# A hybrid attention and FFN block: MLA slots taken in pairs, with the heads' transposes two heads ahead

## The chip, the cores and the metric

The kernel runs on one core of a Trainium2 chip. The metric is the device time of one execution in microseconds (us), the median over several runs. A profile of one execution comes beside it. The engines are TensorE (PE: products and transposes, with its weight loads as PEld), VectorE (DVE), ScalarE (ACT), GpSimd (POOL) and SyncE (SP, which issues most loads). L158 is line 158 of the kernel.

## The reference

One layer on 512 tokens of width 1024, in float32. A normalised x is multiplied by W_in, whose columns feed two groups of attention heads: eight MLA heads, whose queries and keys come out of small latent vectors, and four differential heads. Both attend under a mask by chunks of 64 tokens. A gated FFN with a short convolution and a gated embedding follow. What concerns the change is the MLA group:

```python
    q = rms_norm(q, q_g)
    k = rms_norm(k, k_g)
...
        logits = jnp.einsum('bhqd,bhkd->bhqk', qb, k_t).astype(jnp.float32) * scale
        logits = jnp.where(allowed[None, None], logits, NEG_INF)
        probs = jax.nn.softmax(logits, axis=-1).astype(v_t.dtype)
        return jnp.einsum('bhqk,bhkd->bhqd', probs, v_t)
```

Eight heads (queries and keys of 96 columns, values of 64), and for each the queries in four blocks of 128 tokens. The mask lets block t see the keys of blocks 0 to t only.

## The kernel before, in words

**Number format.** Wide products are made of three: each operand is split into a rounded high part and a low remainder, and `mm3` (L154 to L159) adds high x high, high x low and low x high. A split costs an ACT cast (high) and a DVE subtraction (low): `split` at L182, `lo` at L304, `load_w` at L145.

**MLA slots.** A slot is a head and a query block, (h, t), 32 in all, in the order of `slots` (L727). A slot has these steps:

- `mla_logits` (L564): three products into a `lg` bank, n = 128 (t + 1) columns wide; a DVE maximum over the row and a product with the query's norm; an ACT exponential into a `pm` tile, with the row sum.
- `probs_T` (L535): t + 1 transposes of `pm` into a `tp` bank, then a copy of the bank into a `pt` tile, by DVE for even t and by ACT for odd t.
- `mla_pv` (L578): one product per key block (two records each in the trace) with V, into the bank `mo` of the head pair. After the last slot of a head pair DVE divides by the row sums into `ym`.

Queries and keys of a head are transposed by `mla_q` and `mla_k` (L548, L555) into a `tp` bank and split from there into `QT[h % 2]`: two sets for eight heads.

**Buffers.** PSUM (L112) has banks `acc` 2, `lg` 3, `tp` 2 and `ob` 1. In SBUF there are four `pm` tiles (PM = 4, L50), two `pt` tiles (L124) and five of each weight half (NW = 5). A tile or bank of a tag can be written again once the last reader of the one that held it is done.

**Filling.** `zd_units` (L405) is a generator with 48 units of six products each, the differential group's part of x W_in. `pump(n)` issues the next n. Its first 16 units use the `acc` and `lg` banks ahead of the slots, the others two `acc` banks in turn; after each full sum ACT copies the bank out (L392) and, for queries and keys, squares the tile (L396), and DVE sums the squares (L397). The weights of the second group are loaded by `z1_hi` (L469), the last of them inside the slot loop.

**Order of the work.** PE's instructions run in the order in which the program writes them, throughout (L98). DVE, ACT and POOL do so only inside `region` (L217), which ends in the slot loop at i = 4 (L740); after that a planner orders them by priority and by when their inputs come free. `tc.issue_after(x)` puts what is written inside it behind instruction x on that engine. The loop before takes one slot at a time (L734 to L772): logits of the next slot, in two of four slots the transposes of the next head's queries or keys, one filling unit, the transposes of this slot, the V product of the last one.

**After the slots.** In head 7 the filling changes to the first w_out products (`wo_units`, L642), and `last_mla` (L721) brings the differential group's first transposes (`diff_T`), the transposes of the MLA output (`y_split`) and the loads of x into the last four slots. The differential slots follow (L779).

Of the kernel before, what the change touches and what calls it, by code (L numbers as in the profile page):

```python
# [12 lines left out]
F32R = mybir.dt.float32r  # L13
I32 = mybir.dt.int32
AF = mybir.ActivationFunctionType
ALU = mybir.AluOpType
# [4 lines left out]
P = 128  # L21
T = 512
NT = 4
# [4 lines left out]
H = 8  # L28
# [26 lines left out]
NW = 5  # L55
# [3 lines left out]
FILL_KV = (0, 1, 1, 1)  # L59
FILL_UQ = (1, 1, 1, 1)  # L60
FILL_QK = 5
FILL_MLA = (1, 1, 1, 1)
FILL_DIFF = ((2, 1, 1, 1), (1, 1, 2, 1), (1, 2, 2, 1), (1, 1, 2, 2))

UP_BANKS = ("lg", "tp", "tp", "ob")
# [24 lines left out]
def _f32(ap):  # L90
    return ap.bitcast(F32)
# [3 lines left out]
def hybrid_block(ctx: ExitStack, tc: tile.TileContext, a: dict, out: bass.AP):  # L95
    nc = tc.nc
    V, S, G, TE = nc.vector, nc.scalar, nc.gpsimd, nc.tensor
# [42 lines left out]
    def load_raw(src, n, name):  # L140
        raw = wp["rawpool"].tile([P, 1024], F32, tag="raw", bufs=wp["raw"], name=f"raw_{name}")
        nc.sync.dma_start(raw[:, :n], src)
        return raw
# [106 lines left out]
    for kq in range(4):  # L250
        raw = xn_tile(f"xT{kq}")
# [177 lines left out]
    fill = [zd_units()]  # L429

    def pump(n=1):
        for _ in range(n):
            while fill:
                try:
                    next(fill[0])
                    break
                except StopIteration:
                    fill.pop(0)
# [96 lines left out]
    def probs_T(pm, t, name, on_act):  # L535

        ps = bank("tp", f"pT{name}")
        n = (t + 1) * P
        for j in range(t + 1):
            TE.transpose(ps[:, tsl[j]], pm[:, tsl[j]], ident)  # L540
        pt = pt_tile("pt")
        if on_act:
            S.copy(pt[:, :n], ps[:, :n])
        else:
            V.tensor_copy(pt[:, :n], ps[:, :n])
        return pt

    def mla_q(h):  # L548
        qh_, ql_, kh_, kl_ = QT[h % 2]
        ps = bank("tp", f"qT{h}")  # L550
        for t in range(NT):
            TE.transpose(ps[:QK, tsl[t]], qn[t][:, h, :], ident)
        split(qh_[:QK], ql_[:QK], ps[:QK], qcol[:QK])

    def mla_k(h):  # L555
        qh_, ql_, kh_, kl_ = QT[h % 2]
        ps = bank("tp", f"kT{h}")
        for t in range(NT):
            TE.transpose(ps[:QK, tsl[t]], kv[t][:, h, :QK], ident)
        mla["k"] = split(kh_[:QK], kl_[:QK], ps[:QK])  # L560
# [3 lines left out]
    def mla_logits(h, t):  # L564
        qh_, ql_, kh_, kl_ = QT[h % 2]
        n = (t + 1) * P
        if h % 2 == 0 and t == 0:
            mla["ssum", h // 2] = sm.tile([P, NT, 2], F32, tag="ssum", name="ssum")
        ps = bank("lg", f"ml{h}{t}")
        mm3(ps[:, :n], [(qh_[:100, tsl[t]], ql_[:100, tsl[t]], kh_[:100, :n], kl_[:100, :n])])  # L570
        nm, r = sm.tile([P, 1], F32, tag="nm", bufs=4, name="nm"), rq[:, 0, t, h:h + 1]
        V.reduce_max(nm, ps[:, :n], axis=AX.X, negate=True)  # L572
        mla["nm"] = V.tensor_tensor(nm, nm, r, op=ALU.mult)  # L573
        pm = pm_tile("pm")
        S.activation(pm[:, :n], ps[:, :n], AF.Exp, bias=nm, scale=r, accum_out=mla["ssum", h // 2][:, t, h % 2:h % 2 + 1])  # L575
        mla["pm", h, t] = pm

    def mla_pv(h, t):  # L578
        hp, c = divmod(h, 2)
        if c == 0 and t == 0:  # L580
            mla["po"] = bank("ob", f"mo{hp}")
        po, pt = mla["po"], mla.pop(("pt", h, t))
        w = slice(t * P + 64 * c, t * P + 64 * c + 64)
        for j in range(t + 1):
            TE.matmul(po[:, w], pt[:, tsl[j]], kv[j][:, h, 96:], start=j == 0, stop=j == t)  # L585
        if c == 1 and t == NT - 1:
            rcp = sm.tile([P, NT, 2], F32, tag="rcp", name="rcp")
            V.reciprocal(rcp, mla["ssum", hp])
            yn = tt(f"ym{hp}")
            V.tensor_tensor(yn.rearrange("p (t d) -> p t d", d=64), po.rearrange("p (t d) -> p t d", d=64), rcp.rearrange("p t c -> p (t c)").unsqueeze(2).broadcast_to([P, 8, 64]), op=ALU.mult)  # L590
            ymn.append(yn)
# [3 lines left out]
    def bias_strip():  # L595

        tab = small("tab", [DH, 32])
        nc.sync.dma_start(tab, a["rel_bias"])
        vec1 = dram.tile([DH, NR], F32, name="vec1")
        vec2 = dram.tile([P, DH, NR], F32, name="vec2")  # L600
        vb = sq_tile("vb")[:DH, :NR]
        for c0, c1, b in RUNS:
            G.tensor_scalar(vb[:, c0:c1], tab[:, b:b + 1].broadcast_to([DH, c1 - c0]), -1.0, None, op0=ALU.mult)
        nc.gpsimd.dma_start(vec1, vb)
        nc.gpsimd.dma_start(vec2, vec1.partition_broadcast(P))
        strip = att.tile([P, DH, T], F32, tag="strip", name="strip")
        skew = bass.AP(vec2.tensor, vec2.offset + 127, [[DH * NR - 1, P], [NR, DH], [1, T]])
        nc.gpsimd.dma_start(strip, skew)
        G.memset(strip[:64, :, 448:], MASK)
        strips.append(strip)  # L610
# [4 lines left out]
    def y_split(i, src, col, tag):  # L615

        ps = bank(tag, f"yT{i}")
        for t in range(NT):
            TE.transpose(ps[:, tsl[t]], src[:, tsl[t]], ident)
        yh[i], yl[i] = th_tile(f"yh{i}")  # L620
        df["ysplit"] = split(yh[i], yl[i], ps, col)
# [20 lines left out]
    def wo_units(kq, dqs, nk):  # L642

        for dq in dqs:
            w = wo_w(kq, dq)
            if kq:
                wo2[dq] = w
            for b in (2 * dq, 2 * dq + 1):
                ps = bank("acc", f"o{kq}{b}")
                for k in range(0, nk, 2):  # L650
                    mm3(ps, wo_blocks(4 * kq + k, 4 * kq + k + 2, b, w), k == 0, k == nk - 2)
                    if k == nk - 2:
                        add_x(b, ps)
                    yield

    def diff_T(h, c):
        ps = bank("tp" if h else "acc", f"d{c}T{h}")
        for t in range(NT):
            TE.transpose(ps[:, tsl[t]], zd[c][t][:, h * P:(h + 1) * P], ident)
        h_, l_ = st[4 * (h % 2) + 2 * c], st[4 * (h % 2) + 2 * c + 1]  # L660
        split(h_, l_, ps, dcol if c == 0 else None)
        df["qk", h, c] = (h_, l_)
# [53 lines left out]
    def load_x():  # L716
        for i in range(4):
            x_sb.append(xn_tile(f"x{i}"))
            nc.sync.dma_start(x_sb[i].rearrange("p (k t) -> p k t", t=T), a["xT"][2 * i * P:(2 * i + 2) * P, :].rearrange("(k p) t -> p k t", p=P))

    last_mla = [  # L721
        lambda: diff_T(0, 0),
        lambda: diff_T(0, 1),
        lambda: (y_split(0, ymn[0], None, "acc"), y_split(1, ymn[1], None, "lg"), load_x()),
        lambda: y_split(2, ymn[2], None, "acc"),
    ]
    slots = [(h, t) for h in range(H) for t in range(NT)]  # L727
    mla_q(0)
    pump()
# [1 line left out]
    pump(2)  # L731
    mla_logits(0, 0)
    lo(*z1_[1])
    for i, (h, t) in enumerate(slots):  # L734
        if i < 2:
            (mla_q, mla_k)[t](1)
        if i + 1 < len(slots):
            mla_logits(*slots[i + 1])
        if i == 4:
            region.__exit__(None, None, None)  # L740
            held = tc.issue_after(mla["nm"].ins)
            held.__enter__()
        if i == 8:
            held.__exit__(None, None, None)
            with tc.issue_after(mla["k"].ins):
                zd_norm(0)
        if 0 < h < H - 1 and t < 2:
            (mla_q, mla_k)[t](h + 1)
        if i == 1:
            lo(*z1_hi(3))  # L750
        if i in (9, 11, 13, 15):
            with tc.issue_after(mla["nm"].ins):
                zw2.append(load_w(a["w_d"][2, len(zw2)], 1024, f"d2{len(zw2)}"))
        if h < H - 1:
            pump(FILL_MLA[t])
        if i == 6:
            bias_strip()
        if h == H - 1:
            if t == 0:
                pump(100)  # L760
                fill.append(wo_units(0, range(4), 4))
            last_mla[t]()
            if t == NT - 1:
                raw = load_raw(a["w_out"][0, 0], 1024, "o00")
                hi_o, lo_o = (wts.tile([P, 1024], F32R, tag=i, bufs=NW, name=f"{i}_o00") for i in ("hi", "lo"))
                S.copy(hi_o, raw)
                with tc.issue_after(df["ysplit"].ins):
                    V.tensor_tensor(lo_o, raw, _f32(hi_o), op=ALU.subtract)
                wo_first[0, 0] = (hi_o, lo_o)
        mla["pt", h, t] = probs_T(mla.pop(("pm", h, t)), t, f"m{h}{t}", t % 2)  # L770
        if i:
            mla_pv(*slots[i - 1])  # L772
    diff_logits(0, 0)
    mla_pv(*slots[-1])
    diff_logits(0, 1)
    diff_T(1, 1)
    pump()
# [679 lines left out]
```

## Time and profile before

| | us |
|---|---|
| Median of three runs (lowest, highest) | 648.63 (647.8, 649.95) |
| Time of the profiled execution | 648.05 |
| Its span in the trace | 646.3 |

One execution was profiled. In its rows the first number is the start (or, in a group, the busy time), then the duration; "x4" merges instructions of one kind; a bracket gives the idle time of the engine ahead of the instruction and what ended it. PE's instructions are pipelined: a new one starts before the last one is through, so the cost of one in a stream is the distance between starts, not the duration that its row gives.

### The profile page before, as it was taken

To read this page: it belongs to the slowest core of one execution; us is meant where nothing else is said; L and a number is where in the kernel's file an instruction comes from. 1 tells how busy PE (TensorE), PEld (TensorE's weight loads), DVE (VectorE), ACT (ScalarE), POOL (GpSimd) and SP (SyncE) were. 2 spreads that over 40 slices of the span, in tenths; PEclk is the share of its full clock that TensorE was granted. 3 is DMA by queue.
4 is the path that set the end of the run, shared out by engine and by line. 5 is a ranking of instruction groups with operands and counts; after the bars stand their busy time and mean duration, and the time that the engine had idled before them with its cause. 6 is when DMAs were issued, how large, how long until landed. Compare 5 with 4: busy or idle time off the path is not lost.

```text
span 646.3 us, 10248 instructions
## 1 busy us (share of the span) xinstructions
PE 637.7 (99%) x3916; PEld 567.4 (88%) x3916; DVE 480.9 (74%) x870; ACT 362.3 (56%) x630; POOL 56.0 (9%) x92
## 2 busy tenths in 40 slices
PE   9999999999999999999999999999999999999997
PEld 9988888888787887889999999999999999988886
DVE  6889687646988767888876767677767676769844
ACT  7897666556676465657554555455454545537211
POOL 1510040000000121000100000000001000000000
PEclk9999999999999999999999999999999999999999
DMA  8241225130610428636774646464646463541121
GB/s 308 94 164 51 81 82 165 34 125 20 180 37 2 163 87 255 163 66 180 191 216 114 180 115 187 120 195 119 181 114 180 115 180 115 180 131 52 39 89 50
DMA packets 29912, 82.63 MB, mean 128 GB/s; under 512 B 3100, under 2 KB 4124, under 8 KB 29736
## 3 DMA queue, kind: packets, MB, share of 16 engines
q1 hardware_dynamic: 23816, 69.17, 31.7%
q0 software_dynamic: 5616, 12.33, 11.1%
q8 instruction: 31, 0.51, 0.3%
q10 hardware_dynamic: 432, 0.49, 0.2%
q14 instruction: 17, 0.14, 0.1%
HBM read 77.77 MB, written 5.52 MB: 129 GB/s over the span
## 4 chain that ended last, share of the span: by engine, by line
PE 91%; DVE 5%; ACT 3%; issue 1%; ACTq 0%
PE dn L158 6%; PE dn L157 6%; PE dn L159 6%; PE gx L159 4%; PE gx L158 4%; PE gx L157 4%; PE zd L157 3%; PE zd L159 3%; PE zd L158 3%; PE g L157 3%; PE g L158 3%; PE g L159 3%; PE o L157 3%; PE mo L585 2%; PE o L158 2%; PE pg L157 2%
## 5 line engine op out<-in xcount | busy, mean ns | idle before, releaser
L842 DVE TENSOR_TENSOR wSl<-rS,wSh 128x1024 fp32r<-128x1024 f32 x21 | 25.7, 1224 | 44.5 <-ACT wSh L838 44.3
L157 PE MATMUL dn<-ah,hi_dn 128*128 128x512 f32 x144 | 56.2, 391 | 0.0
L158 PE MATMUL dn<-al,hi_dn 128*128 128x512 f32 x144 | 56.2, 391 | 0.0
L159 PE MATMUL dn<-ah,lo_dn 128*128 128x512 f32 x144 | 56.0, 389 | 0.0
L959 POOL DMA_DIRECT2D rS<-in_w_gu x19 | 22.7, 1195 | 250.1 <-DVE cv L1127 100.7
L838 ACT CAST wSh<-rS 128x1024 fp32r<-128x1024 f32 x21 | 22.1, 1050 | 35.9 <-PE gy L158 35.5
L157 PE MATMUL zd<-hi_d,xh 128*128 128x512 f32 x96 | 39.3, 409 | 0.0
L158 PE MATMUL zd<-lo_d,xh 128*128 128x512 f32 x96 | 37.6, 392 | 0.0
L842 DVE TENSOR_TENSOR wTl<-rA,wTh 128x1024 fp32r<-128x1024 f32 x19 | 23.3, 1225 | 15.2 <-ACT wTh L838 14.7
L633 DVE TENSOR_TENSOR x<-x,dn 128x512 f32<-128x512 f32 x44 | 29.9, 679 | 6.1 <-PE dn L159 6.1
L159 PEld LDWEIGHTS dn<-ah,lo_dn 128*128 128x128 f32 x144 | 27.0, 188 | 5.8
L575 ACT ACTIVATE pm<-ml,nm,rq 128x128 f32<-128x128 f32 (+3 forms) x32 | 19.8, 618 | 21.8 <-DVE nm L573 21.7
L157 PEld LDWEIGHTS dn<-ah,hi_dn 128*128 128x128 f32 x144 | 27.1, 188 | 5.2
L158 PEld LDWEIGHTS dn<-al,hi_dn 128*128 128x128 f32 x144 | 27.1, 188 | 4.9
L572 DVE TENSOR_REDUCE nm<-ml 128x1 f32<-128x128 f32 (+3 forms) x32 | 15.6, 488 | 17.9 <-PE ml L159 17.9
L1130 ACT ACTIVATE cv<-cv 128x512 f32<-128x512 f32 x22 | 13.9, 632 | 24.2 <-DVE cv L1127 24.1
L157 PE MATMUL o<-yh,hi_o 128*128 128x512 f32 x64 | 26.9, 421 | 0.5 <-ACT yh L185 0.5
L838 ACT CAST wAh<-rA 128x1024 fp32r<-128x1024 f32 x21 | 22.1, 1052 | 8.4 <-DMA rA<-in_w_gu 8.2
L157 PE MATMUL g<-b2h,wAh 128*128 128x256 f32 (+1 forms) x88 | 26.4, 300 | 0.3 <-ACT g L1083 0.2
L842 DVE TENSOR_TENSOR wAl<-rA,wAh 128x1024 fp32r<-128x1024 f32 x21 | 25.6, 1218 | 1.3 <-ACT wAh L838 1.3
L159 PE MATMUL g<-b2h,wAl 128*128 128x256 f32 (+1 forms) x88 | 26.2, 297 | 0.0
L158 PE MATMUL g<-b2l,wAh 128*128 128x256 f32 (+1 forms) x88 | 26.2, 297 | 0.0
(478 smaller groups left out, 2218.3 us busy)
## 6 DMA issues: line engine op xcount, KB each, us to landing
rA<-in_w_gu SPq DMA_DIRECT2D x22, 512.0 KB, 3.8
rS<-in_w_gu SPq DMA_DIRECT2D x22, 512.0 KB, 3.6
rS<-in_w_gu POOLq DMA_DIRECT2D x19, 512.0 KB, 6.0
raw_dn<-in_w_down SPq DMA_DIRECT2D x18, 512.0 KB, 5.7
raw_d<-in_w_d SPq DMA_DIRECT2D x12, 512.0 KB, 3.4
r<-in_w_gu SPq DMA_DIRECT2D x19, 256.0 KB, 6.0
raw_o<-in_w_out SPq DMA_DIRECT2D x8, 512.0 KB, 3.6
rS_pg<-in_w_pg SPq DMA_DIRECT2D x6, 512.0 KB, 3.8
```

The source lines that it names most:

```text
L157: TE.matmul(ps, xh, wh, start=first and i == 0, stop=False, skip_group_check=again)
L158: TE.matmul(ps, xh, wl, start=False, stop=False, skip_group_check=again)
L159: TE.matmul(ps, xl, wh, start=False, stop=last and i == n - 1, skip_group_check=again)
L572: V.reduce_max(nm, ps[:, :n], axis=AX.X, negate=True)
L575: S.activation(pm[:, :n], ps[:, :n], AF.Exp, bias=nm, scale=r, accum_out=mla["ssum", h // 2][:, t, h % 2:h % 2 + 1])
L585: TE.matmul(po[:, w], pt[:, tsl[j]], kv[j][:, h, 96:], start=j == 0, stop=j == t)
L633: V.tensor_tensor(xb(b), xb(b), ps, op=ALU.add)
L838: S.copy(h_, src)
L842: V.tensor_tensor(l_, src, _f32(h_), op=ALU.subtract)
L959: nc.gpsimd.dma_start(sums[f].rearrange("p (i c) -> p i c", i=2), a["w_gu"][f][:, :2048].rearrange("p (i c) -> p i c", i=2)[:, :, :512], a ...
L1130: S.activation(cv, cv, AF.Silu)
```

## The change

The slot loop takes two slots at a time. One turn of it (i, i + 1) issues the logits of the next pair, one filling unit in the first turn and two in each later one, the transposes of both slots of this pair, and then the V products of the last pair. At the turn with t = 2 the queries and keys of head h + 2 are transposed behind the V products; those of head 1 are transposed ahead of the loop. The count of filling units is the same. In head 7 the transposes of the differential group come together in the first turn and those of the MLA output in the second, with the first w_out weight's split (`first_o`). Tags and buffer counts are not changed.

```diff
--- before.py
+++ after.py
@@ -59,7 +59,7 @@
 FILL_KV = (0, 1, 1, 1)
 FILL_UQ = (1, 1, 1, 1)
 FILL_QK = 5
-FILL_MLA = (1, 1, 1, 1)
+FILL_PAIR = (1,) + 13 * (2,)
 FILL_DIFF = ((2, 1, 1, 1), (1, 1, 2, 1), (1, 2, 2, 1), (1, 1, 2, 2))
 
 UP_BANKS = ("lg", "tp", "tp", "ob")
@@ -718,12 +718,15 @@
             x_sb.append(xn_tile(f"x{i}"))
             nc.sync.dma_start(x_sb[i].rearrange("p (k t) -> p k t", t=T), a["xT"][2 * i * P:(2 * i + 2) * P, :].rearrange("(k p) t -> p k t", p=P))
 
-    last_mla = [
-        lambda: diff_T(0, 0),
-        lambda: diff_T(0, 1),
-        lambda: (y_split(0, ymn[0], None, "acc"), y_split(1, ymn[1], None, "lg"), load_x()),
-        lambda: y_split(2, ymn[2], None, "acc"),
-    ]
+    def first_o():
+
+        raw = load_raw(a["w_out"][0, 0], 1024, "o00")
+        hi_o, lo_o = (wts.tile([P, 1024], F32R, tag=i, bufs=NW, name=f"{i}_o00") for i in ("hi", "lo"))
+        S.copy(hi_o, raw)
+        with tc.issue_after(df["ysplit"].ins):
+            V.tensor_tensor(lo_o, raw, _f32(hi_o), op=ALU.subtract)
+        wo_first[0, 0] = (hi_o, lo_o)
+
     slots = [(h, t) for h in range(H) for t in range(NT)]
     mla_q(0)
     pump()
@@ -731,11 +734,16 @@
     pump(2)
     mla_logits(0, 0)
     lo(*z1_[1])
-    for i, (h, t) in enumerate(slots):
-        if i < 2:
-            (mla_q, mla_k)[t](1)
-        if i + 1 < len(slots):
-            mla_logits(*slots[i + 1])
+    mla_q(1)
+    mla_logits(0, 1)
+    pump()
+    mla_k(1)
+    for i in range(0, len(slots), 2):
+        h, t = slots[i]
+        pair = slots[i:i + 2]
+        for j in (i + 2, i + 3):
+            if j < len(slots):
+                mla_logits(*slots[j])
         if i == 4:
             region.__exit__(None, None, None)
             held = tc.issue_after(mla["nm"].ins)
@@ -744,34 +752,38 @@
             held.__exit__(None, None, None)
             with tc.issue_after(mla["k"].ins):
                 zd_norm(0)
-        if 0 < h < H - 1 and t < 2:
-            (mla_q, mla_k)[t](h + 1)
-        if i == 1:
+        if i == 0:
             lo(*z1_hi(3))
-        if i in (9, 11, 13, 15):
+        if i in (8, 10, 12, 14):
             with tc.issue_after(mla["nm"].ins):
                 zw2.append(load_w(a["w_d"][2, len(zw2)], 1024, f"d2{len(zw2)}"))
         if h < H - 1:
-            pump(FILL_MLA[t])
+            pump(FILL_PAIR[i // 2])
+        elif t == 0:
+            pump(100)
+            fill.append(wo_units(0, range(4), 4))
         if i == 6:
             bias_strip()
+        for j in pair:
+            mla["pt", *j] = probs_T(mla.pop(("pm", *j)), j[1], f"m{j[0]}{j[1]}", j[1] % 2)
+        for j in slots[i - 2:i] if i else []:
+            mla_pv(*j)
+        if t == 2 and h + 2 < H:
+            mla_q(h + 2)
+            mla_k(h + 2)
         if h == H - 1:
             if t == 0:
-                pump(100)
-                fill.append(wo_units(0, range(4), 4))
-            last_mla[t]()
-            if t == NT - 1:
-                raw = load_raw(a["w_out"][0, 0], 1024, "o00")
-                hi_o, lo_o = (wts.tile([P, 1024], F32R, tag=i, bufs=NW, name=f"{i}_o00") for i in ("hi", "lo"))
-                S.copy(hi_o, raw)
-                with tc.issue_after(df["ysplit"].ins):
-                    V.tensor_tensor(lo_o, raw, _f32(hi_o), op=ALU.subtract)
-                wo_first[0, 0] = (hi_o, lo_o)
-        mla["pt", h, t] = probs_T(mla.pop(("pm", h, t)), t, f"m{h}{t}", t % 2)
-        if i:
-            mla_pv(*slots[i - 1])
+                diff_T(0, 0)
+                diff_T(0, 1)
+                load_x()
+            else:
+                y_split(0, ymn[0], None, "acc")
+                y_split(1, ymn[1], None, "lg")
+                y_split(2, ymn[2], None, "acc")
+                first_o()
     diff_logits(0, 0)
-    mla_pv(*slots[-1])
+    for j in slots[-2:]:
+        mla_pv(*j)
     diff_logits(0, 1)
     diff_T(1, 1)
     pump()
```

## The prediction

> **What bounds the kernel now.** I read the page's busy row first, then the busy time by stretches, then what TensorE (PE) waited for.
>
> ```profile
> span 646.3 us, 10248 instructions
> PE 637.7 (99%) x3916; PEld 567.4 (88%) x3916; DVE 480.9 (74%) x870; ACT 362.3 (56%) x630; POOL 56.0 (9%) x92
> ```
> ```profile
> 62.60:78.00 15.40, 15.19 (x85) 12.46 (x83) 10.64 (x22) 8.78 (x18) 0.00 (x0) 1.00 0.25 78
> 78.00:148.00 70.00, 69.81 (x444) 61.54 (x444) 44.83 (x117) 41.63 (x92) 9.04 (x31) 1.00 0.30 101
> 148.00:166.00 18.00, 16.86 (x121) 14.02 (x119) 13.42 (x34) 12.54 (x32) 0.00 (x0) 1.00 0.20 59
> ```
> ```profile
> PE o L158 <- DVE yh3l L186: 0.6, 1, 0.6
> ...
> PE pTm L540 <- ACT pm L575: 0.5, 2, 0.3
> PE o L157 <- ACT yh L185: 0.5, 1, 0.5
> PE kT L559 <- DVE st L189: 0.2, 1, 0.2
> ```
>
> PE is busy 637.7 of 646.3 us. The MLA slots lie between 62.6 and about 158 us. In their long middle, 78 to 148 us, PE is busy 69.81 of 70.00 at a granted clock of 1.00 and VectorE (DVE) and ScalarE (ACT) have a third of their time free. The four waits shown are all that PE has on the work the change moves: 0.7 us at the transposes (0.2 on kT, 0.5 on pTm) and 1.1 us on the first w_out products just behind the slots. So the stage is bound by the sum of PE's instructions, and a new order can gain only if it makes this sum smaller or takes away some of those 1.8 us.
>
> **Does grouping make the sum smaller?** The change issues the same PE instructions: 48 units of filling products (20 ahead of the loop, then 1 + 13 x 2, then 1, against 19 + 28 + 1), the same transposes and products. Only the order differs. The chain of work gives the period of a head, and the timeline of one head gives prices, as the distance from a start to the next start.
>
> ```profile
> 90.09 0.44 PE pTm L540 x4
> ...
> 148.42 0.44 PE pTm L540 x4
> ```
> ```profile
> 102.94 0.28 PE L159 MATMUL ml<-st 100*128 100x256 f32 x1
> 103.05 0.60 PE L552 MATMUL qT<-ident,qn 128*96 128x128 f32 x4
> ...
> 104.99 1.00 PE L585 MATMUL mo<-kvb,pt 128*128 128x64 f32 x8
> 105.81 0.42 PE L157 MATMUL ml<-st 100*128 100x384 f32 x1
> 106.06 0.34 PE L158 MATMUL ml<-st 100*128 100x384 f32 x1
> 106.24 0.34 PE L159 MATMUL ml<-st 100*128 100x384 f32 x1
> 106.42 0.60 PE L559 MATMUL kT<-ident,kvb 128*96 128x128 f32 x4
> 106.77 0.48 PE L157 MATMUL zd<-hi_d,xh 128*128 128x512 f32 x1
> 107.09 0.39 PE L158 MATMUL zd<-lo_d,xh 128*128 128x512 f32 x1
> 107.32 0.40 PE L159 MATMUL zd<-hi_d,xh0l 128*128 128x512 f32 x1
> ...
> 108.46 0.33 PE L585 MATMUL mo<-kvb,pt 128*128 128x64 f32 x2
> 108.60 0.47 PE L157 MATMUL ml<-st 100*128 100x512 f32 x1
> 108.92 0.39 PE L158 MATMUL ml<-st 100*128 100x512 f32 x1
> ...
> 111.08 0.56 PE L585 MATMUL mo<-kvb,pt 128*128 128x64 f32 x4
> ```
>
> A head takes (148.42 - 90.09) / 5 = 11.67 us. A 512-column product costs 0.23 (107.09 to 107.32), a 384-column one 0.18, a 256-column one 0.11, so a unit of six costs 1.39. At first sight each step from transposes or V products back to logits or filling costs 0.09 more: the zd behind kT takes 0.32, not 0.23. But the four kT took 0.35 up to there, and 0.35 + 0.09 = 0.44, 0.11 each; the surplus is the tail of the group. The V products say the same: mo x8 is four key blocks and costs 0.82 + (0.25 - 0.18) = 0.89, 0.22 a block; mo x2 is one block and costs 0.14 + (0.32 - 0.23) = 0.23. The price goes with the count, and a group has no price of its own. Merging groups therefore takes nothing off the 11.67 us. I put the gain of grouping at 0; the bounds are 0 and the 0.09 of four vanishing steps a head, 8 x 4 x 0.09 = 2.9 us, if the surplus were a price after all. The block prices speak for 0.
>
> **The wait that is added.** Two buffers hold `pt` and two banks hold `tp`, and the change leaves both counts alone. Before, the transposes of slot i were copied out while only slot i-1's `pt` was still to be read. Now a pair is transposed into both banks while the last pair still holds both `pt` buffers: the copy of (h,2) can start only when the product of (h,0) is done, that of (h,3) after (h,1). And right behind those products PE now has `mla_q(h+2)` and `mla_k(h+2)`, which need both banks. PE issues in program order, so all that follows stands behind qT: the next logits and filling. Before, a unit of 1.39 us or more lay in between.
>
> ```profile
> L545 DVE COPY pt<-pTm 128x384 f32<-128x384 f32 x6 | 3.3, 556 | 3.3 <-PE pTm L540 3.3
> ```
> ```profile
> L543 ACT COPY pt<-pTm 128x512 f32<-128x512 f32 x6 | 3.5, 580 | 1.7 <-PE pTm L540 1.6
> ```
> ```profile
> 110.76 0.49 PE L540 MATMUL pTm<-ident,pm 128*128 128x128 f32 x3
> ```
> ```profile
> 111.28 0.56 DVE L545 COPY pt<-pTm 128x384 f32<-128x384 f32 x1
> ```
>
> Count from the end of a pair's filling. The transposes of (h,2) and (h,3) are 7 x 0.11 = 0.77; V products of one and two blocks end their issue at 0.77 + 3 x 0.225 = 1.44, where qT would start. The product of (h,0) ends at 0.77 + 0.33 (row mo x2) = 1.10. The copy follows a PE end by 0.03 (111.25 to 111.28) and takes 0.56, so it ends at 1.69. PE follows DVE by 0.06 (rows below, 70.38 to 70.44): qT at 1.75, 0.31 late. For kT the product of (h,1) ends at 0.995 + 0.56 = 1.55, ACT's copy of 0.58 ends at 2.16, kT can start at 2.22 and qT is through at 1.75 + 0.44 = 2.19: 0.03 more. So **0.34 us a head** with DVE and ACT idle when wanted. They are not always: each is busy some 60% of 78 to 148 us with instructions up to 1.2 us, in order. The lower bound is 0.34; the upper is one such instruction ahead of the copy, 0.34 + 1.2 = 1.5. I take 0.55, near the low end, since in the row above DVE stood idle 3.3 us in all before six such copies, so the copy mostly finds it free. For h = 1 to 5 that is 5 x 0.55 = **2.75 us** (1.7 to 7.5). What it delays is next late itself only in its tail: the splits of q and k have a whole pair (over 5 us of PE work) until the logits of h+2. The logits' three `lg` banks and four `pm` buffers are not late in the middle: an exponential has 4 us or more of PE work before its bank or its transposes are due.
>
> **The start.** Until pair i = 4, DVE and ACT run in program order too, and there the new order costs more.
>
> ```profile
> 69.95 0.27 PE L540 MATMUL pTm<-ident,pm 128*128 128x128 f32 x1
> 70.44 0.64 PE L559 MATMUL kT<-ident,kvb 128*96 128x128 f32 x4 [0.21 <-DVE st L189]
> ...
> 77.62 0.39 PE L159 MATMUL zd<-hi_d,xh7l 128*128 128x512 f32 x1
> 78.20 0.66 PE L540 MATMUL pTm<-ident,pm 128*128 128x128 f32 x4 [0.19 <-ACT pm L575]
> ```
> ```profile
> 73.48 0.67 ACT L575 ACTIVATE pm<-ml,nm,rq 128x384 f32<-128x384 f32 x1 [1.42 <-DVE nm L573]
> ...
> 74.15 1.04 ACT L301 CAST hi_d<-raw_d 128x1024 fp32r<-128x1024 f32 x1
> ...
> 77.28 0.78 ACT L575 ACTIVATE pm<-ml,nm,rq 128x512 f32<-128x512 f32 x1 [0.88 <-DVE nm L573]
> ...
> 78.65 0.68 ACT L392 ACTIVATE zd<-zd,rx 128x512 f32<-128x512 f32 x1
> ```
> ```profile
> 69.63 0.75 DVE L189 SCALAR_TENSOR_TENSOR st<-qT,qcol,st 96x512 fp32r<-96x512 f32 x1
> ...
> 75.22 1.22 DVE L305 TENSOR_TENSOR lo_d<-raw_d,hi_d 128x1024 fp32r<-128x1024 f32 x1 [1.77 <-ACT hi_d L301]
> ...
> 80.02 0.69 DVE L397 TENSOR_REDUCE ssd<-sq 128x8 f32<-128x512 f32 x1 [1.92 <-ACT sq L396]
> ```
>
> Before, PE loses 70.44 - 70.06 = 0.38 at kT and 78.20 - 77.85 = 0.35 at the transposes of (0,3), 0.73 in all; the new order has neither. But the last weight of the second filling group (`z1_hi(3)`) now stands behind two exponentials on ACT instead of one. The exponential of (0,2) ends at 74.15 either way, as the k split ahead of it hangs on DVE; that of (0,3) adds about 0.95, so hi_d starts at 75.1 and lo_d ends near 77.3. PE meanwhile, from kT(1) at 69.95: kT 0.44, logits (0,2) 0.54 and (0,3) 0.69, a unit 1.39, three transposes 0.33, logits (1,0) 0.34: 73.7. Logits (1,1) wait 0.4 for the bank of (0,2), a unit brings PE to 75.9, and the next unit's second product wants that lo_d: 1.2 lost, through at 78.5. Transposes and V products take it to 79.9. The copy of (0,2) stands on DVE behind the sum of squares of this unit's tile, which ends 80.02 + 0.69 - 78.65 = 2.06 after the unit: 80.6; with the copy 81.2, so qT(2) is 1.3 late. Together 2.9 against 0.73: **+2.2 us** (0 if the weight and the sums come as early as before, 3.5 if all waits grow by a fifth).
>
> **The end.** The transposes of (7,3) lose their 0.3 us wait, as the exponentials of the last pair now have a unit and four groups in front. Against that y_split 0, 1 and 2 and the first w_out split come in one bunch, and the first unit of w_out needs `lo_o`, by my count at about the moment it is issued. The 1.1 us on yh3l and yh stay: y_split(3) and its place are the same. I take **0**, between -1.4 (all waits there gone) and +1.2 (one DVE split late). The four loads of x start two slots earlier on SP's queue, at a DMA share of 0.20 in that stretch: 0.
>
> **Sum.** 2.75 + 2.2 + 0 = +4.95 us. The profiled run took 648.05 (span 646.3 and 1.75 around it); it would take 653.0. The median of the runs is 648.63, so 648.63 + 4.95 = **653.6**. PE is the bound afterwards as well (busy 99%), so what the stage loses arrives at the end.
>
> **Rivals.** *The waits all but vanish, no measurable change*: copies always on time, 6 x 0.34 = 2.0 in the ring, the start's 0.73 and the end's 0.3 saved: +1.0, 649.6. For it speaks DVE's idle time before the copies, against it the program order in the start. 15%. *Faster*: grouping does have a price, so 2.9 us come off, and the start and end waits of 1.8 go too, while the ring costs its minimum of 2.0: -2.7, 645.9. It decides if the 0.09 is a price and not a tail; the block prices say tail. 5%. *The copies stand in a queue each time*: 1.5 a head, 5 x 1.5 + 2.2 = +9.7, 658.3; DVE's third of free time speaks against it. 11%. *The clock falls*: if PE were granted half its clock for the rest of a pair (11.67 / 2 = 5.8 us) after each of six waits, +35, 683; 148 to 166 us holds waits of 0.3 to 0.6 us at a granted 1.00, which speaks against it. 2%. The Trainium skill, page "TensorE: Matmul & The Clock Gate", section "A second HAM failure mode: psum-queue depth-cycling", says that short idling between groups which cycle through PSUM banks can make the clock swing; by that rule this rival would be the case, and the trace so far does not bear it out.
>
> **How the numbers follow.** My forecast has 67%. This kernel's measurement can tell about 0.3%, 1.9 us, from no change. Faster by more: 0.05. Within it: the first rival and the forecast's lowest corner, 0.16. Slower: 0.79. The range from 649.4 (first rival) to 657.5 (forecast's upper terms, 1.1 a head and 3.3 at the start) leaves out the faster rival, the clock and most of the queue case.
>
> **What would show it.** Right: among PE's waits, qT on DVE's `pt` copy (L545) in the place of none, about six times and 0.2 to 1 us each; in 80 to 82 us a long one, and zd on lo_d near 76; the head's period 12.0 to 12.5 us instead of 11.67; PE's busy sum unchanged; granted clock 1.00. Wrong: a period under 11.67 (grouping has a price), no waits at qT (a buffer comes free earlier than I read it), or a time under 647.

## The result, and the profile after

The changed kernel takes 657.36 us (median of six executions) against 648.74 us for the kernel before: a ratio of 1.0128, 95% interval 1.0109 to 1.0148. One of the six took 783.99 us at a mean granted clock of 0.754, against 0.995 or more in the five others; the ratio leaves it out, and no trace of it was kept that could tell why. The forecast was 653.6 with a range of 649.4 to 657.5, so the sign was right and the size too small: +8.6 instead of +5.0. The measured time lies only 0.14 us inside the end of the range, and the interval of the ratio reaches past that end: that it fell inside is luck. The profiled execution took 656.26 us, its span is 654.4.

The page's first lines after the change, and PE's waits. A line of the waits gives the waiting line and who released it, then microseconds in all, count, and the longest.

```profile
span 654.4 us, 10227 instructions
PE 640.4 (98%) x3916; PEld 568.9 (87%) x3916; DVE 478.7 (73%) x870; ACT 361.1 (55%) x630; POOL 55.7 (9%) x92
```
```profile
PE qT L552 <- ACT pt L543: 2.2, 3, 0.8
PE kT L559 <- DVE pt L545: 1.4, 2, 0.9
PE warm L201 <- DVE ones L195: 1.1, 1, 1.1
PE pTd L540 <- DVE cf L682: 1.0, 1, 1.0
PE zd L158 <- DVE lo_d L305: 0.8, 1, 0.8
PE qT L552 <- DVE pt L545: 0.6, 3, 0.2
...
PE ml L157 <- ACT pm L575: 0.5, 1, 0.5
...
PE dl L157 <- DVE nmd L677: 0.4, 1, 0.4
```

The same 3916 PE instructions run, and a family of waits that the kernel before did not have is on top: qT and kT, the transposes of the next queries and keys, wait for the copies that empty the two `tp` banks. To see where the 8 us lie, I cut both spans at the same pieces of work: the first qT, the first w_out product, and the column sums (nr) behind the differential slots. The first number pair is the stretch, then its length and PE's busy time in it. The kernel before:

```profile
62.43:161.00 98.57, 97.84 (x629) 85.52 (x628) 64.45 (x159) 58.90 (x128) 9.04 (x31) 1.00 0.26 85
161.00:241.45 80.45, 79.26 (x457) 63.58 (x456) 66.36 (x171) 50.19 (x115) 8.29 (x7) 1.00 0.29 95
```

The changed one:

```profile
62.74:168.64 105.90, 99.90 (x630) 86.64 (x628) 62.34 (x160) 58.34 (x128) 8.89 (x31) 1.00 0.24 78
168.64:249.40 80.76, 79.50 (x458) 63.72 (x456) 66.29 (x170) 50.11 (x115) 8.29 (x7) 1.00 0.29 95
```

The slots take 7.33 us longer, the differential slots 0.31, the way to the first qT 0.31 and all that comes later 0.18: 8.13 in all. The change does not touch the way to the first qT; its length lies between 62.33 and 64.36 us in the traces of this document. The granted clock is 1.00 in both stretches of both executions. Inside the slots, the groups of seven transposes (those of (h,2) and (h,3)) mark the heads. In PE's order of time:

```profile
91.81 0.93 PE L540 MATMUL pTm<-ident,pm 128*128 128x128 f32 x7
...
103.89 0.93 PE L540 MATMUL pTm<-ident,pm 128*128 128x128 f32 x7
...
117.10 0.93 PE L540 MATMUL pTm<-ident,pm 128*128 128x128 f32 x7
...
130.72 0.93 PE L540 MATMUL pTm<-ident,pm 128*128 128x128 f32 x7
...
132.46 0.64 PE L552 MATMUL qT<-ident,qn 128*96 128x128 f32 x4 [0.20 <-DVE pt L545]
132.99 0.64 PE L559 MATMUL kT<-ident,kvb 128*96 128x128 f32 x4
...
142.80 0.93 PE L540 MATMUL pTm<-ident,pm 128*128 128x128 f32 x7
...
154.89 0.93 PE L540 MATMUL pTm<-ident,pm 128*128 128x128 f32 x7
```

The periods are 12.08, 13.21, 13.62, 12.08 and 12.09 us for heads 1 to 5, against 11.67 before: 63.08 - 58.35 = 4.73 us lost in the ring of `pt` buffers and `tp` banks. For the start I compare the first of these groups, at 91.81, with the transposes of (1,3) in PE's timeline of the kernel before:

```profile
89.93 0.60 PE L540 MATMUL pTm<-ident,pm 128*128 128x128 f32 x4
```

At 91.81 the changed kernel has not yet done the transposes of (1,2) and the V products of (1,0) and (1,1), 1.0 us, which the kernel before had behind it at 89.93; it has done the logits of (2,1), 0.34, which that one had not. So it stands where the kernel before stood 0.66 us earlier, and the start cost (91.81 - 62.74) - (89.93 - 0.66 - 62.43) = 2.23. The rest of the 7.33, 0.37, is the end of the slots.

Three heads pay 0.41 us and two pay 1.5 and 1.95. In head 4, a cheap one, the copies on DVE and ACT stand like this:

```profile
131.85 0.56 DVE L545 COPY pt<-pTm 128x384 f32<-128x384 f32 x1 [3.01 <-PE mo L585]
```
```profile
132.35 0.59 ACT L543 COPY pt<-pTm 128x512 f32<-128x512 f32 x1 [0.75 <-PE mo L585]
```

Both engines stand idle and are released by mo, a V product: the transposes were through long before, it is the `pt` buffer that the copy waits for. Now head 2, an expensive one:

```profile
103.67 2.50 DVE L403 TENSOR_TENSOR zd<-zd,rd 128x512 f32<-128x512 f32 x4
106.08 0.68 DVE L397 TENSOR_REDUCE ssd<-sq 128x8 f32<-128x512 f32 x1
106.68 0.55 DVE L545 COPY pt<-pTm 128x384 f32<-128x384 f32 x1
```
```profile
104.81 0.63 ACT L396 ACTIVATE sq<-zd 128x512 f32<-128x512 f32 x1
105.47 0.59 ACT L543 COPY pt<-pTm 128x512 f32<-128x512 f32 x1
```

Here no idle time stands before the copies: on DVE four products of the differential group's norm (`zd_norm`) and a sum are ahead, on ACT the bank copy and square of the filling. ACT's copy is not late by them: it starts 105.47 - 103.89 = 1.58 us behind the first transpose (1.63 in head 4). DVE's starts 2.79 behind instead of 1.13. So qT takes the bank that ACT empties, 0.68 us late, and kT stands another 0.53 us until DVE's copy is done. PE waits for what the planner put first on DVE.

### The profile page after: what moved, and what is told of

Its sections match the earlier page's. It is cut to its first block, busy times and chain, and to the rows that moved or that the text cites. A ratio compares the mean times of both kernels' runs of the same rounds, so it can differ in the third digit from the quotient of the medians.

```text
span 654.4 us, 10227 instructions
## 1 busy us (share of the span) xinstructions
PE 640.4 (98%) x3916; PEld 568.9 (87%) x3916; DVE 478.7 (73%) x870; ACT 361.1 (55%) x630; POOL 55.7 (9%) x92
## 4 chain that ended last, share of the span: by engine, by line
PE 85%; DVE 10%; ACT 3%; issue 1%; ACTq 0%
PE dn L157 6%; PE dn L158 6%; PE dn L159 6%; PE gx L159 4%; PE gx L158 4%; PE gx L157 4%; PE g L157 3%; PE g L158 3%; PE g L159 3%; PE zd L159 3%; PE zd L158 3%; PE zd L157 3%; PE pg L159 2%; PE pg L158 2%; PE pg L157 2%; PE o L157 2%
## 5 line engine op out<-in xcount | busy, mean ns | idle before, releaser
L157 PE MATMUL zd<-hi_d,xh 128*128 128x512 f32 x96 | 37.9, 395 | 0.0
L1362 ACT ACTIVATE sg<-sg 128x512 f32<-128x512 f32 (+1 forms) x9 | 5.3, 584 | 36.8 <-DVE sg L1361 36.8
```

Of the source, the lines that this page charges most:

```text
L157: TE.matmul(ps, xh, wh, start=first and i == 0, stop=False, skip_group_check=again)
L1362: S.activation(sg, sg, AF.Sigmoid)
```

## The experiments

My theory: the waits come from the two `pt` buffers (a copy waits for a V product of the last pair) with q and k right behind; in two heads from `zd_norm` on DVE; at the start from the program order of DVE and ACT. Rivals: a price of grouping on PE itself, or the engines' queues alone. Ratios are to the kernel before, which ran beside each experiment (medians of 648.76 to 649.41 us), with 95% intervals.

**A third `pt` buffer.**

```diff
-        return att.tile([P, T], F32, tag="pt", bufs=2, name=name)
+        return att.tile([P, T], F32, tag="pt", bufs=3, name=name)
```

> The change with three pt buffers instead of two. My theory (the copies wait for the V products of the last pair, and the transposes of q and k stand behind them): with a third buffer the copy of (h,2) starts as soon as it is transposed, so heads 1, 4 and 5 go from 12.08 back to 11.67 us a period, 3 x 0.4; in heads 2 and 3 DVE's copy stands behind the four zd products all the same, so about 0.4 each comes off; the start hardly moves. Together 2 us less than the change: 655.4. Rival, grouping itself has a price on PE: period 12.08 stays, 657.4. Rival, DVE's and ACT's queues alone make the waits: 12.08 stays in heads 1, 4 and 5.

Measured: 652.75 us, 1.0054 (1.0034 to 1.0074). PE's timeline of this run from head 3 on:

```profile
116.30 0.93 PE L540 MATMUL pTm<-ident,pm 128*128 128x128 f32 x7
...
127.86 0.93 PE L540 MATMUL pTm<-ident,pm 128*128 128x128 f32 x7
...
129.24 0.60 PE L552 MATMUL qT<-ident,qn 128*96 128x128 f32 x4
...
139.45 0.93 PE L540 MATMUL pTm<-ident,pm 128*128 128x128 f32 x7
...
151.01 0.93 PE L540 MATMUL pTm<-ident,pm 128*128 128x128 f32 x7
```

The periods of heads 3 to 5 are 11.56, 11.59 and 11.56: the wait is gone, even in head 3 (the two sevens of head 2 are still 13.22 apart). qT follows 1.38 us after the transposes instead of 1.74. The gain is larger than I expected, since head 3 went too: there, with a third buffer, the planner put DVE's copy (at 116.98) ahead of the four products (at 117.45); in head 2 they still stand ahead of it. So the order of DVE's queue hangs in part on the buffers. And 11.56 lies under the 11.67 of the kernel before: grouping does take something off, 0.1 us a head.

**q and k behind the next logits**, without and with the third buffer.

```diff
                 mla_logits(*slots[j])
+        if t == 0 and 0 < h < H - 1:
+            mla_q(h + 1)
+            mla_k(h + 1)
...
-        if t == 2 and h + 2 < H:
-            mla_q(h + 2)
-            mla_k(h + 2)
```

> The change, but the transposes of q and k of the next head come behind the logits of the next turn instead of right behind the V products. My theory: 1.2 us of logits and more then lie between the V products and the transposes that need both tp banks, so the waits at qT and kT go in all six heads (5.9 us in all, with the 1.2 of the start), the period is 11.67, and the time 651.5; 653 if the DVE queue in heads 2 and 3 still reaches over the logits. Rival, grouping itself has a price on PE: 12.08 stays as the least period and the time is over 655.

> Both edits: three pt buffers and the transposes of q and k behind the next logits. My theory: the ring has no wait left to lose but for heads 2 and 3, so this is the later transposes' time less 0 to 1 us, 651, with a period of 11.67 in heads 1, 4 and 5. Rival, grouping has a price: the least period is 12.08, over 655.

Measured: 651.80 us, 1.0041 (1.0025 to 1.0056), and with the third buffer 653.04, 1.0055 (1.0034 to 1.0075), not told apart from it. In both no wait at qT or kT is left, though the first has the old two buffers: it takes the scarce buffers and the place of q and k together to make the wait. The later place removes it in all heads, the third buffer in all but head 2. 651.5 was expected of the first, 651 of the second, which missed it by 2 us. The least period of the first is 11.61 us, so a price of grouping on PE is not what made 12.08. A new wait of 0.6 us in all came in head 1, where the first transposes stand for the splits of q and k.

**The norm's products spread over the turns.** The two groups of four DVE products are kept in a list, and one is issued a turn, behind the logits' bookkeeping.

```diff
+        if zd_todo and i >= 10:
+            with tc.issue_after(mla["nm"].ins):
+                zd_mul(*zd_todo.pop(0))
         if h < H - 1:
             pump(FILL_PAIR[i // 2])
```

> The change with the eight DVE products of the differential group's norm (zd by rd, 128x512) issued one a turn behind the logits' bookkeeping, not four in a row. My theory: in heads 2 and 3 the copy of (h,2) stood behind four of them (2.5 us) on DVE; spread, these heads fall from 13.2 and 13.6 us to 12.1 to 12.4 and the time by 2.3 to 655. Rival, ACT's queue (bank copy and square of the filling ahead of the pt copy) makes those two heads slow: they stay over 13 and the time stays 657.4.

Measured: 653.54 us, 1.0071 (1.0049 to 1.0093). The heads again, in PE's order of time, and the copy of head 2 on DVE:

```profile
104.26 0.93 PE L544 MATMUL pTm<-ident,pm 128*128 128x128 f32 x7
...
116.30 0.93 PE L544 MATMUL pTm<-ident,pm 128*128 128x128 f32 x7
...
128.38 0.93 PE L544 MATMUL pTm<-ident,pm 128*128 128x128 f32 x7
```
```profile
104.04 0.69 DVE L407 TENSOR_TENSOR zd<-zd,rd 128x512 f32<-128x512 f32 x1
105.40 0.56 DVE L549 COPY pt<-pTm 128x384 f32<-128x384 f32 x1 [0.66 <-PE mo L589]
```

Heads 2 and 3 fall from 13.21 and 13.62 to 12.04 and 12.08, the level of the others, and DVE waits for mo again. The products in a row were the difference; the ACT queue did not keep these heads slow. The five heads together lose 2.71 us less, where 2.3 was expected; the time fell further, below the 655 expected, and the trace does not show by what.

**The start, two ways.** The cast of `z1_hi(3)` ahead of the loop; and, apart from it, `region` ended ahead of the loop.

```diff
     mla_k(1)
+    z13 = z1_hi(3)
     for i in range(0, len(slots), 2):
...
-            lo(*z1_hi(3))
+            lo(*z13)
```

> The change with the cast of the last weight of the second filling group issued ahead of the loop, before the two exponentials of (0,2) and (0,3) on ACT. My theory of the start: the wait of 0.8 us (1.0 by starts) at the filling product on lo_d goes, all else stays, so 1.0 us less than the change, 656.4. Rival, the start's loss is all in the copy behind the sum of squares: the wait at lo_d goes but qT(2) waits so much longer, 657.4.

```diff
+    region.__exit__(None, None, None)
     for i in range(0, len(slots), 2):
...
         if i == 4:
-            region.__exit__(None, None, None)
```

> The change with the stretch in which DVE and ACT run in program order ended ahead of the slot loop instead of at i = 4. My theory of the start: the copy of (0,2) need not stand behind the sum of squares of the filling's tile, so the wait at qT(2) falls from 1.2 us to the 0.4 of the later heads, and the weight's split may come earlier as well: 1 to 2 us less than the change, 655.8. Rival, the buffers hold this wait too and not the order: qT(2) waits as before, 657.4.

Measured: 655.95 us, 1.0117 (1.0096 to 1.0138), and 655.67, 1.0108 (1.0088 to 1.0127). By time alone neither is told apart from the changed kernel, whose interval they overlap; the traces decide. With the early cast the wait on lo_d is gone, part of it comes back at the logits, and the first seven transposes stand 78.69 - 63.23 = 15.46 us behind the first qT instead of 78.96 - 62.74 = 16.22:

```profile
75.48 0.38 PE L157 MATMUL ml<-st 100*128 100x256 f32 x1 [0.91 <-ACT pm L575]
78.69 0.93 PE L540 MATMUL pTm<-ident,pm 128*128 128x128 f32 x7
```

With the program order ended early, qT(2) waits 0.20 instead of 0.78, for DVE's copy released by mo as in the later heads: the order held the longer wait there, not the buffers. The weight's split comes early as well (at 71.32 instead of 76.42), so the wait on lo_d is gone here too; a wait of 0.47 at the transposes of (0,1) is new.

```profile
79.51 0.93 PE L540 MATMUL pTm<-ident,pm 128*128 128x128 f32 x7
81.25 0.64 PE L552 MATMUL qT<-ident,qn 128*96 128x128 f32 x4 [0.20 <-DVE pt L545]
```

**All remedies together**: three buffers, spread norm, early cast, early end of the program order; then also with q and k behind the logits.

> Paired slots with all the waits taken away that I have found: three pt buffers, the zd products spread over the turns, the last weight cast early, and the program-order stretch ended ahead of the loop. My theory: of the 8.6 us the ring (4.7) and the start (2.2) go, what is left is 0 to 1 us over the kernel before, ratio 1.000, with a period of 11.56 us a head. Rival, pairing delays DVE and ACT in the differential slots behind it: 2 us and more over the kernel before stay (ratio 1.003 or more) though the slots run at 11.6.

> As the run with all waits taken away, and the transposes of q and k behind the next logits as well. My theory: nothing is left for it to take away in the middle, so the same time within 0.5 us; at the start the transposes of (1,0) and (1,1) may wait for the split of q and k, 0.6 us, as in the run with later transposes. Rival: the place of q and k matters by itself, over 1 us either way.

Measured: 648.99 us, 1.0006 (0.9996 to 1.0015), and 649.04, 1.0002 (0.9989 to 1.0016). The whole loss is gone, and pairing the slots is worth nothing that can be measured. (The remedies were not tried on the kernel before, whose own idle time on PE in the slots is 0.73 us.) The two stretches of the first of them, and the longest of its waits inside them:

```profile
63.05:161.24 98.19, 97.66 (x629) 86.20 (x628) 61.92 (x159) 57.46 (x128) 8.89 (x31) 1.00 0.27 85
161.24:242.00 80.76, 79.54 (x458) 63.74 (x457) 66.28 (x170) 50.15 (x115) 8.29 (x7) 1.00 0.29 95
```
```profile
176.78 0.63 PE L544 MATMUL pTd<-ident,pmd 128*128 128x128 f32 x4 [0.98 <-DVE cf L686]
```

The slots take 0.38 us less than in the kernel before; the periods of heads 1 and 3 to 5 are 11.56 to 11.59, that of head 2 is still 11.89. The differential slots take 0.31 of it back. The two waits of the kernel before at the w_out products are gone, and instead the differential transposes wait a full microsecond while DVE splits three w_out weights in a short time:

```profile
172.08 2.35 DVE L151 TENSOR_TENSOR lo_o<-raw_o,hi_o 128x1024 fp32r<-128x1024 f32 x2
...
174.75 1.22 DVE L151 TENSOR_TENSOR lo_o<-raw_o,hi_o 128x1024 fp32r<-128x1024 f32 x1
```

**An attempt at that wait**, on the mended pairs and on the kernel before: the DVE splits of those w_out weights of the first group (kq = 0) that are loaded after the fourth differential slot's logits are put behind the probabilities of a differential slot (`fin` lists the last instruction of each).

```diff
-        return load_w(a["w_out"][kq, dq], 1024, f"o{kq}{dq}")
+        if len(fin) < 4 or kq:
+            return load_w(a["w_out"][kq, dq], 1024, f"o{kq}{dq}")
+        with tc.issue_after(fin[-3].ins):
+            return load_w(a["w_out"][kq, dq], 1024, f"o{kq}{dq}")
```

> The run with all waits taken away, and the DVE splits of the w_out weights put behind the probabilities of the differential slot that is transposed next, so that two or three of them (1.2 us each) no longer stand ahead of those. My theory: what the paired slots gain (0.1 us a head, and the waits at the old start) is given back in one wait of 1.0 us at the differential transposes; without it the kernel is 0.5 to 1.2 us under the kernel before, ratio 0.9985. Rival: the wait only moves to the w_out products, which then stand at the split, ratio 1.000 or more.

> The kernel before with that same edit of the w_out splits alone. Theory: before, the two waits at the w_out products (1.1 us in all) come from the order of DVE's queue too, a w_out split ahead of yh3l, so 0 to 1.1 us come off, ratio 0.999, and the mended pairs' lead over this is within 0.5 us. Rival: no wait of the kernel before hangs on these splits, ratio 1.000.

Measured: 652.11 us, 1.0047 (1.0035 to 1.0059), and 653.97, 1.0078 (1.0062 to 1.0094). Both are slower, where a gain was expected. The waits aimed at did shrink: on the mended pairs the 0.98 at pTd is gone, and on the kernel before the two at the w_out products fall from 0.47 and 0.57 to 0.17 and 0.22. But in both kernels a later pTd waits 0.37 and 0.55 for a copy on ACT, and near the end of the differential slots a longer wait came: a w_out product stands until DVE has added an earlier one to x. The first run's rival came nearest, though the wait moved to the bank that x's sum frees and not to the split. The mended kernel's line:

```profile
219.39 0.50 PE L157 MATMUL o<-yh,hi_o 128*128 128x512 f32 x1 [2.32 <-DVE x L637]
```

In the other it is 2.41. The trace of the second run is of its fastest execution, 651.56 us, so half of its loss stands in no trace. So nothing that I ran beats the kernel before. What order of DVE's queue there would suit the paired slots stays open.

## Why the prediction was right, and where its size was off

**PE bounds the stage, and a new order cannot gain much: right.** With nearly every wait of the slots removed, the time is that of the kernel before.

**Grouping gains 0: nearly.** The period without waits is 11.57 and not 11.67 us, so about a tenth a head; over eight heads I estimate 0.8 us from it; the slots of the run with all remedies are 0.38 us shorter, with the waits that are left in them. Of the 0.09 us that each of four steps a head seemed to cost, at most some 0.025 (0.1 over four) is a price, an estimate too, and the rest was the tail of the group, as the block prices had said.

**The wait added: right in its mechanism and in its clockwork.** The copy of (h,2) was forecast 1.13 us behind the first of the seven transposes, qT 1.75 and ACT's copy 1.58; in head 4 they came 1.13, 1.74 and 1.63 behind. The least cost was forecast as 0.34 a head and is 0.41 on the old period, 0.51 on the period that the third buffer shows. Of the signs that I had named, the period of 12.0 to 12.5 us came in three heads of five, and qT stood for DVE's copy only three times, 0.20 each; at the start and in heads 2 and 3 it stood 0.68 to 0.78 for ACT's copy, and kT in heads 2 and 3 then 0.53 and 0.90 for DVE's.

**Its mean was the step that failed.** I took 0.55 a head; the five heads cost 0.95 on average, 4.73 instead of 2.75. I had read DVE's idle time before the copies of the old order as a sign that it would be free, and had bounded the worst case, 1.5 a head, by one instruction of 1.2 us; head 3 paid 1.95. In two heads a row of four products, 2.5 us, stood ahead, in head 2 a sum as well. In the old order the row was not ahead of a copy that PE waited for: of the first four products only one stood right ahead of a copy, 0.69 at 87.89, and the second four ran at 113.94, when the copy of (3,2) was over (111.28 and 0.56). But the row was there to be seen in the kernel (`zd_norm`, released at i = 8 and after the second filling group), and I should have laid it over the turns.

**The start: right**, 2.23 for 2.2. Logits (1,1) waited 0.52 for their bank (0.4 forecast), the filling product 0.76, by starts 1.0, on lo_d (1.2), and q and k of head 2 came 1.2 late (1.3 forecast): kT starts 81.99 - 78.96 = 3.03 us behind the seven transposes, against 1.82 in the later heads of the run with three buffers.

**The end: mis-sized, 0 forecast, 0.37 measured.** One wait of 0.43 came at the second pair of differential logits, whose bank was freed late on DVE behind the three y splits and the w_out split in a bunch; it lies inside the bounds that I gave. The two waits at yh3l and yh did not stay, as I had said, but went; a wait of 1.0 at the differential transposes came in their place. These nearly cancel; the stretch is 0.31 longer, and of that the trace books 0.24 as busy time of PE.

**PE's busy sum did not stay the same**, as I had written, but rose by 2.7 us. The profile models PE's ends, and an instruction ahead of or behind a wait is drawn longer (qT 0.64 for 0.60): the lost time is only partly booked as idle. Distances between starts show all of it.

**The rivals.** The rival of no measurable change had the copies always on time, which held in three heads of five; but the start cost 2.23 where that rival had it gain 0.73. A price of grouping exists, about 0.1 us a head where that rival needed 0.36 (2.9 over eight heads). The queue rival (1.5 a head throughout) was true of two heads in five. The clock stayed at 1.00 in the slots of the profiled execution. The Trainium skill, page "TensorE: Matmul & The Clock Gate", section "A second HAM failure mode: psum-queue depth-cycling", tells of another kernel, whose clock swung because PE often idled briefly while cycling through PSUM banks. PE did idle so in the profiled execution here, 0.2 to 0.9 us once or twice a head, and the clock did not move.

## What to carry to other kernels

When steps are batched, count the buffers that are alive at the moment of the batch, not on average: here two slots at a time wanted a third `pt` tile where one at a time did with two (a fourth was not tried). Look at what stands right behind the step that frees a buffer; putting independent work there (the next logits) served as well as another buffer. Look also at long runs of instructions on the engine that makes the copy, and lay them over the new order. And where PE already runs without gaps, an order that only regroups its instructions has almost nothing to win, while the waits that it brings arrive at the end: of the 8.13 us here 7.33 came in the slots.

## What the runs showed of the hardware that was not expected

What a scarce buffer costs hangs on what is queued ahead of the copy that it holds up: with the same two buffers, a head cost 0.41 us where DVE stood idle and 1.5 to 1.95 us where four products of 0.6 us each were ahead. The Trainium skill, page "Perfetto Trace Analysis", section "Optimization Strategy", names a gap that repeats on the engine that should be saturated as a possible sign of too few buffers. That holds here, with 0.41 us a head gone by a third buffer, but the repeated gap was the smaller half of the 4.73 us, 5 x 0.41 = 2.05; the other 2.68 went when the products were spread. The two causes are not apart, though: the third buffer freed head 3 of its row as well, and the later place of q and k removed the waits at qT and kT in every head without touching the products.
